# First head's output gate as a fifth column tile of the raw-input stage, with the small weights loaded later and the first head's decays and the recurrences' start steps renumbered

## The chip, the core and the metric

The kernel runs on one core of one Trainium2 chip. The metric is the device time of one execution in microseconds (us), as the median of several runs. The profile of one further execution, with all engines' instructions, is what the prediction reads. The engines are called by their short names: PE (TensorE, matrix products), PEld (its weight loads), DVE (VectorE), ACT (ScalarE), POOL (GpSimd) and SP (SyncE, which here only issues transfers); SPq, ACTq and POOLq are the queues from which transfers are issued.

## The reference, cut to what matters

One residual block on x of shape 512 x 1024. Two token mixers run side by side on the normalised input: a gated delta rule with eight heads of 128, and a convolution module. Then come merging gates and a SwiGLU channel mixer.

```
h = rmsnorm(x, norm1_w)
q, k, v, z, b_raw, a_raw, glu, gates = split(h @ w_in)
q, k, v = silu(causal_conv4([q, k, v]));  q, k = l2norm(q), l2norm(k)
beta = sigmoid(b_raw);  g = -exp(A_log) * softplus(a_raw + dt_bias)
o = gated_delta_rule(q, k, v, g, beta)          # per head, in chunks
out_a = (rmsnorm(o, dn_norm_w) * silu(z)) @ dn_w_o
ga, gb = split(glu + b_glu);  c = causal_conv31(ga * sigmoid(gb))
out_b = silu(layernorm(c)) @ cm_w_pw2
x = x + (gate_a * out_a + gate_b * out_b) @ w_out
x = x + (silu(f_gate) * f_up) @ ffn_w_down      # f from rmsnorm(x)
```

`z` is the gate of the heads' outputs, 128 columns for each head. `b_raw` and `a_raw` are 16 columns in all, and every head's decay and beta come from them.

## The kernel before, in words

All large products are done in three terms: each operand is split into a high and a low part, and `split3` (L112 to L118) issues high by high, high by low and low by high. `unit` (L98 to L110) loads 128 x 1024 weights with SP into `raw` (L105), makes the high part `whi` on ACT (L108) and the low part `wlo` on DVE (L109). These three tiles come from the pool `wp`, three buffers each, so a conversion has to wait until PE is through with the unit three before. One projection `proj(j)` is one unit and 24 matmuls of 128 x 512 on L118, given out in eight steps of three.

**The raw-input stage** (L205 to L302). The first four column tiles (the halves of the first two GLU pairs) are multiplied with the input before it is normalised, since the norm is one factor for each token that can be applied behind the product. `xt` comes in eight slices; ACT makes `uh` (L254), DVE makes `ul` (L255), and for every second slice three quarters of weights are converted (L260, L261). The 16 columns of `b_raw` and `a_raw` are done in the same loop (L265, L266) with the weights `wb`, which SP loads (L230) and DVE splits (L246, L247). Meanwhile the norm's factor `rsb` is made. Then the fourth tile is done alone (PSUM tile `b`), and the normalised input `hh` (ACT L299) and `hl` (DVE or POOL in turns, L300) is written slice by slice.

**The decays** (L304 to L339, L701 to L719). From the 16 columns DVE and ACT make `g` (written on L335) and `beta` in a chain of about 20 small operations. `decays` is a generator that starts two steps into the projections: it multiplies `g` with constant masks on PE (L707), takes exponentials on ACT, multiplies again (L714), copies the result on ACT into `mr` (L716, tile `cv`), and SP writes that to memory (`mrow`, L718). `decay(h)` reads a row of it back for head h, broadcast to 128 partitions (tile `DT`, L391), and makes the mask of decays on POOL and ACT (L393, L396).

**A head.** `head` (L721) projects and convolves k, q and v, and projects z (L737). `front` (L399) builds the triangular matrix of the head (`Un`, L422), writes its small diagonal blocks to memory and reads them back broadcast (SP, `sc` L437 and `U` L440), and POOL inverts these 16 x 16 blocks in 15 pairs of dependent operations (L454, L456; result `y`). `chain` then works from `y`: six small groups of matmuls on PE (L490, L496, L514, L522, L534, L539), with copies on DVE or ACT between them, give the whole inverse; four recurrence steps follow, each with L552/L553 (state), L555 (DVE, `R`), L558, L560 (ACT, `w`), L563/L564 and L570 (DVE, the new state). Everything in a chain depends on the piece before it.

**What sets the order.** The projections of heads and other tiles stand in a queue and are taken step by step (L665, `count`). `chains` holds the generators of `decays` and of the heads' `chain`; a number that a generator yields is the count of steps until it goes on. A head's chain is put in at step `START + 32 h + ...` (L771). That gives the program order with priorities; a scheduler at build time then sets the final order of each engine, within the dependences and its own estimate of readiness. `behind` and `issue_after` keep some operations behind others: POOL's part of `front` for head h + 1 stands behind the last operation of head h's inversion (`last`). On the chip each engine works through its own list in order, so that an instruction which waits holds up all behind it. `conv31` (L620, 30 operations on DVE for each of eight tiles, the first ACT L618 and the last ACT L622) fills DVE.

Of the kernel before, what the change touches and what calls it, by code (L numbers as in the profile page):

```python
# [14 lines left out]
P = 128  # L15
T = 512
NT = 4
# [4 lines left out]
OFF = 1600  # L22
PAD = 416
PAD3 = 368
START = 84
ROUND = 40
OTHERS = (12, 12, 12, 12, 8, 8, 8, 8)
EPS = 1e-6
# [3 lines left out]
def block_kernel(ctx, tc, a):  # L32
# [176 lines left out]
    with tc.tile_pool(name="st", bufs=2) as st:  # L209
# [5 lines left out]

        early = [[p.tile([P, 1024], dt, name=n, **kw) for dt, n in ((F32, "raw"), (F32R, "whi"), (F32R, "wlo"))]
                 for p, kw in ((wp, {}), (wp, {}), (st, {}), (st, {}))]
        nc.sync.dma_start(vec, a["vec"])
        nc.scalar.dma_start(ident, a["cst"][:, 0:P])

        def load(u, q):
            s = slice(256 * q, 256 * q + 256)
            nc.sync.dma_start(early[u][0][:, s], a["win"][(40, 32, 41, 33)[u]][:, s])

        for q in range(4):
            nc.sync.dma_start(xt[:, 2 * q, :], a["xt"][2 * q])
            load(0, q)
            nc.sync.dma_start(xt[:, 2 * q + 1, :], a["xt"][2 * q + 1])
            if q == 0:
                nc.sync.dma_start(wb, a["wba"])  # L230
            for u in (1, 2):
                load(u, q)
        xtok = pa_.tile([P, NT, D], F32, name="A")
        for n in range(NT):
            nc.sync.dma_start(xtok[:, n, :], a["x"][n])
# [7 lines left out]
        tc.cur_priority = prio  # L243
        wbhl = wbs[:, 0:2 * P].rearrange("p (k i c) -> p k i c", k=KD, i=2)
        wbh, wbl = wbhl[:, :, 0, :], wbhl[:, :, 1, :]
        V.tensor_copy(out=wbh, in_=wb)  # L246
        V.tensor_tensor(out=wbl, in0=wb, in1=wbh.bitcast(F32), op=ALU.subtract)  # L247


        bps = psg.tile([P, T], F32, name="g")  # L250
# [1 line left out]
        for k in range(KD):  # L252
            w = vec[:, k:k + 1]
            S.activation(uh[:, k, :], xt[:, k, :], AF.Copy, scale=w)  # L254
            V.scalar_tensor_tensor(out=ul[:, k, :], in0=xt[:, k, :], scalar=w, in1=uh[:, k, :].bitcast(F32),  # L255
                                   op0=ALU.mult, op1=ALU.subtract)
            if k % 2 == 0:
                c = slice(k * P, k * P + 256)
                for raw, hi, lo in early[:3]:
                    S.activation(hi[:, c], raw[:, c], AF.Copy)  # L260
                    V.tensor_tensor(out=lo[:, c], in0=raw[:, c], in1=hi[:, c].bitcast(F32), op=ALU.subtract)  # L261
            c = slice(k * P, k * P + P)
            for (_, hi, lo), ps in zip(early[:3], eps_):
                split3(ps, (hi[:, c], lo[:, c]), uh[:, k, :], ul[:, k, :], k == 0, k == KD - 1)
            PE.matmul(bps[0:32, :], wbs[:, 32 * k:32 * k + 32], uh[:, k, :], start=k == 0, stop=False)  # L265
            PE.matmul(bps[0:16, :], wbs[:, 32 * k:32 * k + 16], ul[:, k, :], start=False, stop=k == KD - 1)  # L266
        ss = st.tile([P, 2, NT], F32, name="rms_ss", bufs=1)
        for n in range(NT):
            S.activation(xtok[:, n, :], xtok[:, n, :], AF.Square, scale=1.0 / 32, accum_out=ss[:, 0, n:n + 1])
# [11 lines left out]
        for k in range(KD):  # L281
            c = slice(k * P, k * P + P)
            split3(eps_[3], (hi[:, c], lo[:, c]), uh[:, k, :], ul[:, k, :], k == 0, k == KD - 1)
        def glu0(i):
            sg = tp.tile([P, T], F32, name="sg")
            V.tensor_tensor(out=sg, in0=eps_[2 * i], in1=rsb, op=ALU.mult)
            S.activation(sg, sg, AF.Sigmoid, bias=b_glu[:, 8 + i:9 + i])
            c = tp.tile([P, T + 30], F32, name="c", bufs=3)
            V.memset(c[:, 0:30], 0.0)
            V.tensor_tensor(out=c[:, 30:], in0=eps_[2 * i + 1], in1=rsb, op=ALU.mult)  # L290
            V.scalar_tensor_tensor(out=c[:, 30:], in0=c[:, 30:], scalar=b_glu[:, i:i + 1], in1=sg,
                                   op0=ALU.add, op1=ALU.mult)
            cs.append(c)
# [13 lines left out]
        for n in range(NT):  # L307
# [24 lines left out]
        V.tensor_tensor(out=t0, in0=t0, in1=u, op=ALU.mult)  # L332
        V.tensor_tensor(out=sp, in0=sp, in1=t0, op=ALU.subtract)
        V.scalar_tensor_tensor(out=sp, in0=ax, scalar=0.0, in1=sp, op0=ALU.max, op1=ALU.add)
        V.tensor_tensor(out=g, in0=sp, in1=nea.rearrange("p (a h) -> p a h", a=1).broadcast_to([P, NT, H]),  # L335
                        op=ALU.mult)
        V.tensor_scalar(out=eb, in0=eb, scalar1=1.0, scalar2=None, op0=ALU.add)
        V.reciprocal(out=beta, in_=eb)
        V.tensor_scalar(out=nbeta, in0=beta, scalar1=-1.0, scalar2=None, op0=ALU.mult)  # L339


    gp = ph1.enter_context(tc.tile_pool(name="gp", bufs=1))
# [33 lines left out]
        yield  # L376
        return o

    zall = pa_.tile([P, H, T], F32, name="A")
    junk = tp.tile([P, T], F32, name="pa", bufs=1)  # L380

    def tok(src, pool, tag):
# [317 lines left out]

    def decays():  # L701

        yield 2
        gps = psg.tile([P, 4, P], F32, name="g")
        fl = lambda t: t.rearrange("p n h -> p (n h)")
        for i, m in enumerate((tri, suf, ones, mid)):
            PE.matmul(gps[:, i, 0:32], m, fl(g), start=True, stop=True)  # L707
        S.activation(fl(egc), gps[:, 0, 0:32], AF.Exp)
        S.activation(fl(kdf), gps[:, 1, 0:32], AF.Exp)
        S.activation(fl(egl), gps[:, 2, 0:32], AF.Exp)  # L710
        V.tensor_scalar(out=negc, in0=egc, scalar1=-1.0, scalar2=None, op0=ALU.mult)
        V.tensor_scalar(out=fl(nmc), in0=gps[:, 3, 0:32], scalar1=-1.0, scalar2=None, op0=ALU.mult)
        mps = psg.tile([P, 4, P], F32, name="g")
        PE.matmul(mps[0:32, 0, :], fl(g), mid, start=True, stop=True)  # L714
        mr = mrt[0:32, 0:P]
        S.activation(mr, mps[0:32, 0, :], AF.Copy)  # L716
        for n in range(NT):
            nc.sync.dma_start(mrow[:, n, :], mr[n * H:(n + 1) * H])  # L718
        dts.append(decay(0))  # L719

    def head(h, done):  # L721

        k_ = yield from conv4(8 + h, "kT")
        close()
        q_ = yield from conv4(h, "qT")
        close()
        v = conv4(16 + h, "vT")
        for _ in range(2):
            next(v)
            yield  # L730
        DT = dts.pop(0)
        if h + 1 < H:
            dts.append(decay(h + 1))
        with behind(), tc.issue_after(last[0].ins) if h else nullcontext():
            ss, kd, b2, Un, Ud, y = front(h, k_, DT)
        v_ = yield from v
        pz = yield from proj(24 + h)  # L737
        z_ = zall[:, h, :]
        S.activation(z_, pz, AF.Silu)

# [27 lines left out]
    nh = 0  # L768
    while step() or chains:
        start_feed[0] = count[0] >= 335  # L770
        if nh < H and count[0] >= START + 32 * nh + sum(OTHERS[:nh]):  # L771
            chains.append([0, chain(*done[nh])])
            nh += 1
        for c in list(chains):
            if c[0] <= count[0] or not queue:
                with behind():
                    n = next(c[1], None)
                if n is None:
                    chains.remove(c)
                else:  # L780
                    c[0] = count[0] + n
# [515 lines left out]
```

## Time and profile before

| what | us |
|---|---|
| median of three runs | 963.14 |
| lowest and highest run | 960.74, 963.42 |
| the profiled execution | 964.17 |
| its span in the trace | 961.9 |
| PE busy | 941.8 (98%) |
| DVE busy | 731.8 (76%) |
| ACT busy | 529.4 (55%) |
| POOL busy | 357.4 (37%) |

Of the profiled execution 2.3 us lie outside the span. Rows of the timeline read: start in us, duration in us, engine, line, operation, the tile written and the tile read, partitions x elements, and a count where like rows in a run are put together. In brackets at the end stands how long the engine sat idle before, and what ended that. Matmuls are pipelined, so that a matmul's duration is longer than the distance to the next start; that distance, the pitch, is what counts. A matmul of plain 32-bit numbers shows as two records (x8 for four of them), a three-term matmul of L118 as one.

### The profile page before, as it was taken

Reading aid. Unit: us, or ns where it says so; the run is one execution under the profiler, and the core shown is the slowest. Engines: PE = TensorE matmul, PEld = TensorE weight load, DVE = VectorE, ACT = ScalarE, POOL = GpSimd, SP = SyncE. Lnnn points to the kernel's source line nnn. Section 1 sums busy time; section 2 is a strip of 40 time slices with the busy share of each in tenths; the row PEclk is TensorE's granted clock in tenths of the full one; section 3 lists DMA queues with packets and bytes.
Section 4 is the critical chain, followed back from the end, with each engine's and each line's share of the span. In section 5 each row is a group of like instructions: output and inputs, shape, how many; then the busy total and the mean of one; then the engine's idle time right before and its main releaser. Section 6 shows DMA issues by size and latency. Waiting matters only on the chain.

```text
span 961.9 us, 14869 instructions
## 1 busy us (share of the span) xinstructions
PE 941.8 (98%) x5199; PEld 793.8 (83%) x5199; DVE 731.8 (76%) x1118; ACT 529.4 (55%) x1095; POOL 357.4 (37%) x565
## 2 busy tenths in 40 slices
PE   6999999999999999999999999999999999999996
PEld 5687888888887887888887888888889999988885
DVE  4898888988888888888477763676525887889886
ACT  6588865867856775544547232423324545556554
POOL 0323645243463327534345342245451111134034
PEclk9999999999999999999999999999999999999999
DMA  9243423133231426988897985499899556578653
GB/s 310 94 143 101 123 66 92 59 116 102 66 103 55 129 82 176 279 253 248 257 297 221 288 277 175 174 272 281 294 252 224 191 184 193 174 221 268 212 192 134
DMA packets 78298, 177.39 MB, mean 184 GB/s; under 512 B 10208, under 2 KB 19328, under 8 KB 77200
## 3 DMA queue, kind: packets, MB, share of 16 engines
q1 hardware_dynamic: 66816, 144.88, 45.4%
q0 software_dynamic: 10256, 28.89, 13.3%
q10 hardware_dynamic: 1152, 2.69, 0.7%
q8 instruction: 41, 0.67, 0.3%
q14 instruction: 33, 0.27, 0.1%
HBM read 156.22 MB, written 45.37 MB: 210 GB/s over the span
## 4 chain that ended last, share of the span: by engine, by line
PE 90%; DVE 4%; ACT 2%; POOL 2%; issue 1%; DMA 1%; SPq 0%; POOLq 0%; ACTq 0%; DVEq 0%
PE mm L118 59%; PE w L118 20%; PE g L385 1%; PE st L564 1%; PE g L418 1%; PE st L558 1%; DVE wlo L109 1%; PE b L490 1%; PE st L563 1%; PE b L496 1%; DMA gsl<-sgd 1%; POOL ss L879 1%; PE b L514 1%; PE st L552 1%; PE g L467 1%
## 5 line engine op out<-in xcount | busy, mean ns | idle before, releaser
L108 ACT ACTIVATE whi<-raw 128x1024 fp32r<-128x1024 f32 (+1 forms) x191 | 196.4, 1030 | 246.8 <-PE mm L118 151.1
L109 DVE TENSOR_TENSOR wlo<-raw,whi 128x1024 fp32r<-128x1024 f32 (+1 forms) x191 | 242.3, 1270 | 95.9 <-ACT whi L108 95.3
L118 PE MATMUL mm<-hh,whi 128*128 128x512 f32 (+1 forms) x688 | 269.9, 393 | 0.5 <-ACT whi L108 0.3
L118 PE MATMUL mm<-hl,whi 128*128 128x512 f32 (+1 forms) x688 | 264.0, 384 | 2.3 <-POOL hl L300 1.6
L118 PE MATMUL mm<-hh,wlo 128*128 128x512 f32 (+1 forms) x688 | 263.9, 384 | 0.1
L620 DVE SCALAR_TENSOR_TENSOR cps<-c,c31w,cps 128x512 f32<-128x512 f32 x240 | 180.2, 751 | 4.3
L118 PEld LDWEIGHTS mm<-hl,whi 128*128 128x128 f32 x688 | 129.9, 189 | 24.7 <-POOL hl L300 2.9
L118 PEld LDWEIGHTS mm<-hh,wlo 128*128 128x128 f32 x688 | 129.6, 188 | 23.8 <-DVE wlo L109 0.6
L118 PEld LDWEIGHTS mm<-hh,whi 128*128 128x128 f32 x688 | 129.8, 189 | 22.7 <-ACT whi L108 0.8
L949 POOL TENSOR_TENSOR fm<-fm 128x256 f32<-128x256 f32 x33 | 29.8, 904 | 113.3 <-DVE s L949 90.1
L372 DVE SCALAR_TENSOR_TENSOR acc<-mm,c4w,acc 128x511 f32<-128x511 f32 (+2 forms) x72 | 53.0, 738 | 1.9 <-ACT acc L369 1.9
L118 PE MATMUL mm<-yh,whi 128*128 128x512 f32 x128 | 50.7, 396 | 0.0
L118 PE MATMUL mm<-yl,whi 128*128 128x512 f32 x128 | 50.0, 391 | 0.6 <-DVE yl L808 0.6
L454 POOL TENSOR_TENSOR ytm<-U,y 128x60 f32<-128x60 f32 (+14 forms) x120 | 31.8, 265 | 48.6 <-DMA U<-sc 30.9
L118 PE MATMUL mm<-yh,wlo 128*128 128x512 f32 x128 | 49.8, 389 | 0.0
L118 PE MATMUL w<-hh,wlo 128*128 128x256 f32 x168 | 47.7, 284 | 0.3 <-DVE wlo L109 0.3
L118 PE MATMUL w<-hh,whi 128*128 128x256 f32 x168 | 47.6, 284 | 0.0
L118 PE MATMUL w<-hl,whi 128*128 128x256 f32 x168 | 47.5, 283 | 0.0
L118 PE MATMUL w<-wlo,fh 128*128 128x512 f32 (+1 forms) x115 | 44.3, 385 | 0.2 <-DVE wlo L109 0.2
L118 PE MATMUL w<-whi,fl 128*128 128x512 f32 (+1 forms) x115 | 44.2, 384 | 0.0
L118 PE MATMUL w<-whi,fh 128*128 128x512 f32 (+1 forms) x115 | 44.2, 384 | 0.0
L456 POOL TENSOR_TENSOR y<-y,ytm 128x60 f32<-128x60 f32 (+14 forms) x120 | 39.0, 325 | 9.4
(324 smaller groups left out, 1904.0 us busy)
## 6 DMA issues: line engine op xcount, KB each, us to landing
raw<-in_win_dram SPq DMA_DIRECT2D x61, 512.0 KB, 3.5
raw<-in_wgu_dram SPq DMA_DIRECT2D x32, 512.0 KB, 3.5
s<-in_wgu_dram SPq DMA_DIRECT2D x48, 256.0 KB, 6.2
raw<-s SPq DMA_DIRECT2D x48, 256.0 KB, 3.8
raw<-wsum SPq DMA_DIRECT2D x44, 256.0 KB, 4.0
raw<-in_wdn_dram SPq DMA_DIRECT2D x33, 256.0 KB, 3.3
s<-in_wgu_dram POOLq DMA_DIRECT2D x24, 256.0 KB, 6.9
s<-s POOLq DMA_DIRECT2D x24, 256.0 KB, 7.0
```

The costliest lines, as they stand in the source:

```text
L108: marked(S.activation(hi, raw, AF.Copy), "unit")
L109: marked(V.tensor_tensor(out=lo, in0=raw, in1=hi.bitcast(F32), op=ALU.subtract), "unit")
L118: marked(PE.matmul(ps, l, r, start=first and i == 0, stop=last and i == 2))
L372: marked(V.scalar_tensor_tensor(out=acc[:, s:], in0=ps[:, :T - s], scalar=c4w[:, j, k:k + 1], in1=acc[:, s:], op0=ALU.mult, op1=ALU.add))
L385: PE.transpose(ps[:, n, :], src[:, n, :], ident)
L418: PE.matmul(ps[:, n, :], kT[:, n, :], kT[:, n, :], start=True, stop=True)
L454: G.tensor_tensor(out=tm[:, :, 0:w], in0=U[:, k, :, k + 1:], in1=y[:, :, k:k + 1].broadcast_to([P, NT, w]), op=ALU.mult)
L456: last[0] = G.tensor_tensor(out=y[:, :, k + 1:], in0=y[:, :, k + 1:], in1=tm[:, :, 0:w], op=ALU.add)
L467: PE.matmul(ps[:, n, :], kT[:, n, :], qT[:, n, :], start=True, stop=True)
L490: PE.matmul(ps[:, n, 0:16], Ud[:, n, :], xc[:, n, 0:16], start=True, stop=True)
L620: V.scalar_tensor_tensor(out=acc, in0=c[:, k:k + T], scalar=c31w[:, i, k:k + 1], in1=acc, op0=ALU.mult, op1=ALU.add)
L949: return eng.tensor_tensor(out=out, in0=in0, in1=in1, op=op)
```

## The change

- `vec` is loaded from ACT's queue and not SP's, so that the first slice of `xt` is SP's first transfer. `wb` is loaded after the three quarters of weights of the first round, and its split on DVE stands in the loop's second pass. The matmuls with it follow two slices later, so that PE's first instruction is a projection on L118.
- Column tile 24 (z of head 0) becomes a fifth tile on the raw input, into the PSUM tile `st`, straight behind the fourth. DVE multiplies it with `rsb` behind the operation that writes `g`, and ACT applies Silu. Head 0 has no z projection any more, and is eight steps shorter.
- `decays` starts twelve steps into the projections and not two.
- `START` is 80 and not 84, and heads 1 to 7 get four steps off, for the steps that head 0 no longer has.

```diff
-START = 84
+START = 80
...
-        nc.sync.dma_start(vec, a["vec"])
+        nc.scalar.dma_start(vec, a["vec"])
...
+            for u in (1, 2):
+                load(u, q)
             if q == 0:
                 nc.sync.dma_start(wb, a["wba"])
-            for u in (1, 2):
-                load(u, q)
...
-        V.tensor_copy(out=wbh, in_=wb)
-        V.tensor_tensor(out=wbl, in0=wb, in1=wbh.bitcast(F32), op=ALU.subtract)
...
-            PE.matmul(bps[0:32, :], wbs[:, 32 * k:32 * k + 32], uh[:, k, :], start=k == 0, stop=False)
-            PE.matmul(bps[0:16, :], wbs[:, 32 * k:32 * k + 16], ul[:, k, :], start=False, stop=k == KD - 1)
+            if k == 1:
+                V.tensor_copy(out=wbh, in_=wb)
+                V.tensor_tensor(out=wbl, in0=wb, in1=wbh.bitcast(F32), op=ALU.subtract)
+            for b in [k - 2] if 1 < k < KD - 1 else [k - 2, k - 1, k] if k > 1 else []:
+                PE.matmul(bps[0:32, :], wbs[:, 32 * b:32 * b + 32], uh[:, b, :], start=b == 0, stop=False)
+                PE.matmul(bps[0:16, :], wbs[:, 32 * b:32 * b + 16], ul[:, b, :], start=False, stop=b == KD - 1)
...
+        zps = pst.tile([P, 4, P], F32, name="st").rearrange("p n t -> p (n t)")
+        hi, lo = unit(a["win"][24])
+        for k in range(KD):
+            c = slice(k * P, k * P + P)
+            split3(zps, (hi[:, c], lo[:, c]), uh[:, k, :], ul[:, k, :], k == 0, k == KD - 1)
+        zall = pa_.tile([P, H, T], F32, name="A")
...
+        with tc.issue_after(g_.ins):
+            V.tensor_tensor(out=zall[:, 0, :], in0=zps, in1=rsb, op=ALU.mult)
+        S.activation(zall[:, 0, :], zall[:, 0, :], AF.Silu)
...
-        yield 2
+        yield 12
...
-        pz = yield from proj(24 + h)
         z_ = zall[:, h, :]
-        S.activation(z_, pz, AF.Silu)
+        if h:
+            pz = yield from proj(24 + h)
+            S.activation(z_, pz, AF.Silu)
...
-        if nh < H and count[0] >= START + 32 * nh + sum(OTHERS[:nh]):
+        if nh < H and count[0] >= START + (32 * nh - 4 if nh else 0) + sum(OTHERS[:nh]):
```

The final order of the engines moves further than the diff says. The first place is ACT's list around the copy of the decays, `cv_99<-g` 32x128 (`mr`). In the kernel before it stands on L716, right behind the last exponential of the decays, with six weight conversions (L108) of `unit` ahead of it in the list:

```order
L710 ACTIVATE sm_414<-g_488 128x32
L716 ACTIVATE cv_99<-g_498 32x128
L375 ACT_TABLE_LOAD
L375 ACTIVATE vT_780<-acc4_775 128x512
L405 ACTIVATE pa_454,ss_659<-g_660 128x128
L739 ACTIVATE A_453<-mm_782 128x512
```

In the changed kernel the same copy stands on L728, behind the end of the second tile's 31-tap convolution (L634, before L622):

```order
L752 ACTIVATE A_398<-mm_1557 128x512
L108 ACTIVATE whi_1847<-raw_1846 128x1024
L634 ACTIVATE cv_102<-cps_576 128x512
L728 ACTIVATE cv_99<-g_642 32x128
L382 ACTIVATE acc4_1832<-mm_1747,c4w_79 128x512
L108 ACTIVATE whi_1902<-raw_1901 128x1024
```

So 19 weight conversions of `unit` now stand ahead of the copy. The matmul that feeds it (L714, now L726) has hardly moved on PE: 187 matmuls of L118 were ahead of it, and now 180 are. The first chain's first matmul on PE (L490, now L502) had 354 matmuls of L118 ahead of it and now has 631, the second chain's 487 and now 672, the third's 618 and now 707.

The second place is PE's list in the recurrences of head 0. In the kernel before, pieces of a chain stand between matmuls of the projections (`hh`, `hl` with `whi`, `wlo`), as here in one recurrence step of head 0, where `st_1532<-R` and the `st_1532<-w` that waits for it have six of these between them:

```order
L118 MATMUL mm_1559<-hl_92,whi_1561 128x512
L118 MATMUL mm_1559<-hh_91,wlo_1562 128x512
L558 MATMUL st_1532<-R_1535,Y_437 128x128
L118 MATMUL mm_1559<-hh_91,whi_1561 128x512
L118 MATMUL mm_1559<-hl_92,whi_1561 128x512
L118 MATMUL mm_1559<-hh_91,wlo_1562 128x512
L118 MATMUL mm_1559<-hh_91,whi_1561 128x512
L118 MATMUL mm_1559<-hl_92,whi_1561 128x512
L118 MATMUL mm_1559<-hh_91,wlo_1562 128x512
L563 MATMUL st_1532<-w_1547,kd_669 128x128
L564 MATMUL st_1532<-w_1547,at_848 128x128
```

In the changed kernel the last three steps of head 0 stand without a projection between them, and the first matmul of head 1's chain (L502) follows in the same stretch:

```order
L118 MATMUL mm_2336<-hh_91,wlo_2339 128x512
L570 MATMUL st_1542<-R_1545,Y_471 128x128
L575 MATMUL st_1542<-w_1571,kd_702 128x128
L576 MATMUL st_1542<-w_1571,at_849 128x128
L564 MATMUL st_1600<-S_1584,kT_541 128x128
L565 MATMUL st_1600<-S_1584,qT_670 128x128
L570 MATMUL st_1600<-R_1603,Y_471 128x128
L575 MATMUL st_1600<-w_1622,kd_702 128x128
L576 MATMUL st_1600<-w_1622,at_849 128x128
L564 MATMUL st_1695<-S_1661,kT_541 128x128
L565 MATMUL st_1695<-S_1661,qT_670 128x128
L502 MATMUL b_1700<-xc_1671,Ud_1039 128x16 x4
```

Behind the last row the stretch goes on without a projection through all six small groups of head 1's inverse, to L551 (before L539). The next projection's matmul (`mm_2397`) comes after that, with no matmul of L118 between it and `mm_2336`.

More of the change, by code (lines that the diff above doesn't have):

```diff
@@ L334, in block_kernel @@
         V.scalar_tensor_tensor(out=sp, in0=ax, scalar=0.0, in1=sp, op0=ALU.max, op1=ALU.add)
-        V.tensor_tensor(out=g, in0=sp, in1=nea.rearrange("p (a h) -> p a h", a=1).broadcast_to([P, NT, H]),
+        g_ = V.tensor_tensor(out=g, in0=sp, in1=nea.rearrange("p (a h) -> p a h", a=1).broadcast_to([P, NT, H]),
                         op=ALU.mult)
@@ L377, in conv4 @@
         return o
-    zall = pa_.tile([P, H, T], F32, name="A")
     junk = tp.tile([P, T], F32, name="pa", bufs=1)
```

## The prediction

> **What bounds the kernel now.** I read the page first, then the list of waits with PE's own rows, then the timelines around the edits, and last the build order shown above. The page's engine line, its chain by engine and the longest waits of PE:
>
> ```profile
> PE 941.8 (98%) x5199; PEld 793.8 (83%) x5199; DVE 731.8 (76%) x1118; ACT 529.4 (55%) x1095; POOL 357.4 (37%) x565
> ...
> PE 90%; DVE 4%; ACT 2%; POOL 2%; issue 1%; DMA 1%; SPq 0%; POOLq 0%; ACTq 0%; DVEq 0%
> ```
>
> ```profile
> PE g L265 <- DVE cv L247: 7.2, 1, 7.2
> PE mm L118 <- POOL hl L300: 1.6, 2, 1.3
> ...
> PE mm L118 <- DVE hl L300: 0.6, 1, 0.6
> ```
>
> PE is the bound: 941.8 of 961.9 us busy. The change takes no matmul away (the z tile moves, all 24 remain), so only PE's idle time can move, and of the 20.1 us that are idle 7.2 lie before the first matmul and 2.2 in two names of one stall. What the change could gain is small. What it could lose is any wait that it makes on PE, since each stands one to one in the time. Therefore I look for new waits as carefully as for removed ones.
>
> **The start.** The timeline of the first microseconds, with PE's pitch until it quickens:
>
> ```profile
> 0.73 0.40 SPq L218 DMA_DIRECT2D vec<-in_vec_dram  x1
> ...
> 1.18 0.42 SPq L226 DMA_DIRECT2D xt<-in_xt_dram  x1
> ...
> 4.14 1.28 ACT L254 ACT_TABLE_LOAD   x1 [4.14 <-DMA xt<-in_xt_dram]
> ...
> 5.44 0.72 ACT L254 ACTIVATE uh<-xt,vec 128x512 fp32r<-128x512 f32 x1
> ...
> 6.07 0.40 ACT L260 ACTIVATE whi<-raw 128x256 fp32r<-128x256 f32 x1
> ...
> 7.22 0.61 PE L265 MATMUL g<-uh,cv 128*32 128x512 f32 x1 [7.22 <-DVE cv L247]
> ...
> 7.63 0.63 PE L118 MATMUL mm<-uh,whi 128*128 128x512 f32 x1
> ...
> 12.75 0.63 PE L118 MATMUL mm<-uh,wlo 128*128 128x512 f32 x1
> 13.17 0.44 PE L118 MATMUL mm<-uh,whi 128*128 128x512 f32 x1
> 13.45 0.40 PE L118 MATMUL mm<-ul,whi 128*128 128x512 f32 x1
> ```
>
> `vec` off SP's queue lets `xt` go one slot earlier (0.73 in place of 1.18), 0.45 us. ACT's chain of table load, `uh` and `whi` follows it: `whi` ended at 6.47 and would end at 6.02, and PE, whose first product is now on L118, would start 0.13 later for its weights, at about 6.15 and not 7.22. That is **-1.1**. Moving `wb` and its split costs nothing there, as the first product with it comes 27 matmuls later. The pitch is 0.42 up to 13.17 and then about 0.24 (0.28 for the first). If the quickening stays at 13.17, only the 2.5 matmuls that fit into 1.07 us are gained at the fast pitch, 0.6; if all 13 slow matmuls were fast, 13 x 0.19 = 2.5 would come on top of 1.1. So -0.6 to -3.6; I take the plain shift, since the transfers of the next slices set these rows as well.
>
> The Trainium skill ("TensorE: Matmul & The Clock Gate", Part 1) says that the clock opens after a busy window of about 3.4 us that runs free of the kernel's start; by that the gain here would be the 0.6, or about 2.8 if a whole window were saved.
>
> **The z tile over the stall.** PE's rows where the normalised input is written:
>
> ```profile
> 37.08 0.50 PE L118 MATMUL mm<-hh,whi 128*128 128x512 f32 x1
> ...
> 41.34 0.50 PE L118 MATMUL mm<-hl,whi 128*128 128x512 f32 x1 [1.29 <-POOL hl L300]
> ...
> 46.29 0.50 PE L118 MATMUL mm<-hl,whi 128*128 128x512 f32 x1 [0.36 <-POOL hl L300]
> ...
> 46.85 0.40 PE L118 MATMUL mm<-hh,whi 128*128 128x512 f32 x1
> ```
>
> A long undisturbed piece of the chain that ended last, for the pitch, and the last piece of `hl`:
>
> ```profile
> 91.44 11.17 PE mm L118 x49
> ```
>
> ```profile
> 44.94 1.29 POOL L300 TENSOR_TENSOR hl<-xt,hh 128x512 fp32r<-128x512 f32 x1 [1.96 <-ACT hh L299]
> ```
>
> The undisturbed pitch is 11.17 / 49 = 0.228. From 37.08 to 46.85 PE took 27 steps, so 6.2 of the 9.8 us were work and 3.6 a stall, more than the 2.2 in the list of waits, since small gaps aren't listed. The 24 matmuls of the z tile, 5.5 us, need no `hl` and now stand there. With the start 1.1 earlier, PE would come to the first `hh` product at about 41.4 and to the last slice of `hl` at 46.4. The z tile's weight conversion (L109) also stands on DVE ahead of the `hl` chain, which ended at 46.23 and would end at about 46.5 (1.1 earlier for the start, 1.3 later for the conversion). So nearly all of the stall is covered: **-3.5** (0 if the chain slips by as much as the tile takes, -3.6 at most).
>
> **The wait for g.** DVE's chain from the sixteen columns to `g`, PE's reader, and the mean durations of what stands between on DVE:
>
> ```profile
> 45.92 0.21 DVE L309 COPY cv<-g 128x64 f32<-128x64 f32 x1
> ...
> 60.82 0.19 DVE L335 TENSOR_TENSOR cv<-cv 128x32 f32<-128x32 f32 x1
> ```
>
> ```profile
> 61.40 0.97 PE L707 MATMUL g<-cv,cst 128*128 128x32 f32 x8
> 62.30 0.41 PE L714 MATMUL g<-cst,cv 128*32 128x128 f32 x2
> ```
>
> ```profile
> L109 DVE TENSOR_TENSOR wlo<-raw,whi 128x1024 fp32r<-128x1024 f32 (+1 forms) x191 | 242.3, 1270 | 95.9 <-ACT whi L108 95.3
> L620 DVE SCALAR_TENSOR_TENSOR cps<-c,c31w,cps 128x512 f32<-128x512 f32 x240 | 180.2, 751 | 4.3
> L372 DVE SCALAR_TENSOR_TENSOR acc<-mm,c4w,acc 128x511 f32<-128x511 f32 (+2 forms) x72 | 53.0, 738 | 1.9 <-ACT acc L369 1.9
> ```
>
> PE was just behind `g` (61.01 against 61.40). The changed PE list has 60 matmuls of L118 between the first `hh` product and the reader, where it had 91: 41.4 + 60 x 0.228 = 55.1. DVE's new list has between the same two ends two L109, ten of the 0.75 us kind and 16 small ones: 2.5 + 10 x 0.66 (they overlap a little) + 16 x 0.1 (the next starts while one ends) = 10.7, from about 46.4, so 57.1. PE waits **+2** (0 to 4); the projection after it in PE's list stands behind this wait.
>
> **The late copy of the decays.** The chain before, from the copy to the first two inversions and the first chain's matmul:
>
> ```profile
> 62.74 0.27 ACT L716 ACTIVATE cv<-g 32x128 f32<-32x128 f32 x1
> ```
>
> ```profile
> 91.26 0.99 POOL L454 TENSOR_TENSOR ytm<-U,y 128x60 f32<-128x60 f32 x1 [8.96 <-DMA raw<-in_win_dram]
> ...
> 102.56 0.21 POOL L456 TENSOR_TENSOR y<-y,ytm 128x4 f32<-128x4 f32 x1
> ...
> 129.20 0.21 POOL L456 TENSOR_TENSOR y<-y,ytm 128x4 f32<-128x4 f32 x1
> ...
> 162.50 0.21 POOL L456 TENSOR_TENSOR y<-y,ytm 128x4 f32<-128x4 f32 x1
> ```
>
> ```profile
> 108.35 0.96 PE L490 MATMUL b<-xc,Ud 128*128 128x16 f32 x8
> ```
>
> From the copy at 62.74 to `y` of head 0 (102.77) it was 40.0 us, to head 1's another 26.6, and from the start of POOL's part for head 2 (the row below) to the end of its `y` 24.6:
>
> ```profile
> 138.15 1.04 POOL L412 TENSOR_TENSOR ss<-ss,root 128x4 f32<-128x4 f32 x1 [8.74 <-DVE ss L410]
> ```
>
> In the new list the copy stands behind 19 weight conversions and the end of a 31-tap convolution. The last of these conversions needs PE to be through with the projection three units before, which has 480 matmuls of L118 ahead of its end, 300 of them after the reader of `g`: 57.1 + 300 x 0.228 + some 4 for the small groups between, at up to 1 us each as L707's row has it, = 130. Then one conversion on ACT (1.1), one on DVE (1.3), the six last taps (6 x 0.66) and two short ACT copies: 136.9. The way from there to `y` of head 0 took 40 us; POOL's 8.96 us of waiting at 91.26, put down to a load of weights, may shrink, so 35 to 40, and I take 35: **172**. Heads 1 and 2 follow 26.6 and 24.6 later, since their part of POOL stands behind the inversion before: 198.6 and 223.2. What lies between `y` and the chain's first matmul is two ACT copies and a transpose; I take 3 us (5.6 at 108.35).
>
> PE's own arrival, by its list at the pitches above: at the first chain 172, at the second 190, at the first projection behind the bare stretch 196.4, at the third chain 209.4. Against the readiness of 175, 201.6 and 226.2, PE waits 3 at the first and stands some 17 later at the third. Part of this is the bare stretch itself, where a recurrence step takes its full latency:
>
> ```profile
> 143.13 0.39 PE L552 MATMUL st<-S,kT 128*128 128x128 f32 x2
> 144.18 0.49 PE L558 MATMUL st<-R,Y 128*128 128x128 f32 x2
> 145.13 0.49 PE L563 MATMUL st<-w,kd 128*128 128x128 f32 x2
> ```
>
> Between these rows lie 1.05 and 0.95 us for 0.45 of PE's work, and no projection hides it now. The two accounts overlap (the wait for `y` runs beside the recurrence), and give the same: 201.6 at head 1's first matmul, then its bare inverse of six groups (0.8 to 0.9 us each, an estimate from the 0.96 of L490) and five hops (0.95 as above, up to 1.6 where several copies stand between, an estimate), 9.5 to 13 us, so PE is at the next projection at 211 to 215 and not 196.4. I take **+16.5** (from +5.6, if only hops count and `y` is never late, to +22 with 40 us to the first `y`). Behind the stretch I add **+1** for weights whose loads SP issues behind this stretch's transfers. ACT gets five more table loads (5 x 1.28), hidden as it is 55% busy.
>
> **The sum:** -1.1 - 3.5 + 2 + 16.5 + 1 = +14.9 against the profiled 964.17, hence 979.1. That execution lies 1.0 above the median of the runs, 963.14, so I predict **978**.
>
> **The rivals.**
>
> *The recurrences stay covered (not slower).* If the inversions of heads 1 and 2 follow within 15 us of the one before, `y` is there whenever PE comes, and only the start's and z tile's gains stand against the wait for `g`: -4.6 + 2, 960 to 963. For it: ACT's part of `front` can be ready long before, as the projections run ahead. Against: the 26.6 and 24.6 us above are POOL's own list and its transfers. It decides at 15 us of period. 12 in 100, half under 960.2.
>
> *A smaller stall.* The hops count but POOL's period falls to 18, since transfers have less before them: third chain ready at 172 + 36 + 3 = 211 against 209.4, bare hops +5.6, in all +3 to +8: 966 to 971. 18 in 100.
>
> *PE's clock falls in the stretch.* PE would then be idle for about 6 us in one piece (own arrival and hops 195.5, `y` 201.6). The longest idle time that the rows above show behind the start is 1.29, and the pitch after it is as before, so the trace can't tell. If PE came back at the pitch of the start, 0.42, for as long as it did there (5.5 us), it would cost about 2.5 more: 980 to 984. 20 in 100. The Trainium skill (same page and Part) has the clock halved after one idle window of about 3.4 us; the trace neither shows nor excludes it.
>
> **The numbers.** The forecast, 972 to 982 without that clock, has 50 in 100. The range of 966 to 985 leaves out the first rival and a little at the top, where 40 us to `y` and the clock come together. About 0.3% (2.9 us) is what a measurement of this kernel can tell from no change: faster 0.06, same 0.07, slower 0.87.
>
> **What would show it.** Right: PE's first matmul at about 6.2 on L118; no `hl` wait over 0.5; a wait of PE for `g` of about 2; ACT's copy L728 near 137; `y` of head 0 near 172; and a list of waits with some 15 us on the chain's lines (L502, L526, L570, L575) between 172 and 215. Wrong: the copy before 100, or the second `y` less than 18 after the first.

## The result, and the profile after

The changed kernel takes 985.76 us (median of 4 runs, 985.41 to 988.63), the kernel before 963.03 in the runs beside it (4 runs, 960.74 to 963.42). The ratio is 1.0241, with a 95% interval of 1.0213 to 1.0269: slower by 2.4%. The forecast was 978 with a range of 966 to 985. The direction and the late copy came out; PE's path behind the copy did not, and the time is 7.8 us above the forecast and 0.8 above the range. The profiled execution has a span of 983.4 where the kernel before had 961.9, 21.5 more.

The page's engine line and the chain by engine, as shown of the kernel before:

```profile
PE 949.5 (97%) x5199; PEld 804.8 (82%) x5199; DVE 740.0 (75%) x1119; ACT 535.0 (54%) x1100; POOL 351.8 (36%) x561
...
PE 83%; POOL 5%; DVE 3%; DMA 3%; issue 2%; ACT 2%; SPq 1%; POOLq 0%; ACTq 0%; DVEq 0%
```

PE is busy 7.7 us longer with the same 5199 matmuls, so part of them ran slower, and it is idle 13.8 us longer. POOL has 5% of the chain where it had 2%, and DMA 3% where it had 1%: the chain now passes through the inversions. The longest waits of PE:

```profile
PE mm L118 <- ACT whi L258: 6.1, 1, 6.1
PE st L564 <- DVE o L589: 4.0, 2, 2.2
PE g L397 <- ACT pa L484: 2.9, 1, 2.9
PE mm L118 <- ACT sg L616: 1.9, 1, 1.9
PE g L719 <- issue: 1.9, 1, 1.9
PE g L479 <- ACT Un L433: 1.7, 1, 1.7
```

The wait at the start is shorter, those for `hl` are gone, the wait for `g` (L719) is there with 1.9, and the other four lines are new. Three of these are waits for ACT (L397, L118 and L479, 6.5 in all) and were not in the forecast. Of the 15 us or so that the forecast put on L502, L526, L570 and L575 between 172 and 215 only 1.6 are there.

The start, the first product of the normalised input and the reader of `g`, on PE's timeline:

```profile
6.08 0.79 PE L118 MATMUL mm<-uh,whi 128*128 128x512 f32 x1 [6.08 <-ACT whi L258]
...
10.13 0.40 PE L118 MATMUL mm<-uh,whi 128*128 128x512 f32 x1
...
40.57 0.50 PE L118 MATMUL mm<-hh,whi 128*128 128x512 f32 x1
...
56.38 1.05 PE L719 MATMUL g<-cv,cst 128*128 128x32 f32 x8 [1.92 <-issue]
...
57.70 0.65 PE L118 MATMUL mm<-hh,whi 128*128 128x512 f32 x1
58.15 0.63 PE L118 MATMUL mm<-hl,whi 128*128 128x512 f32 x1
58.58 0.63 PE L118 MATMUL mm<-hh,wlo 128*128 128x512 f32 x1
```

PE starts at 6.08 (forecast 6.15) and quickens at 10.13, not at 13.17. Less the z tile's 24 matmuls (5.5 us) the first product of `hh` is at 35.1, 2.0 earlier than before. The reader of `g` waits 1.92 as forecast. What was not forecast is the row behind it: the pitch is 0.43 and not 0.228. PE runs at half speed for the next eight matmuls.

ACT's late copy and the ends of the first three inversions on POOL:

```profile
130.21 1.06 ACT L108 ACTIVATE whi<-raw 128x1024 fp32r<-128x1024 f32 x1 [3.89 <-PE mm L118]
137.37 0.60 ACT L634 ACTIVATE cv<-cps 128x512 f32<-128x512 f32 x1 [6.10 <-DVE cps L632]
137.86 0.25 ACT L728 ACTIVATE cv<-g 32x128 f32<-32x128 f32 x1
```

```profile
173.27 1.09 POOL L468 TENSOR_TENSOR y<-y,ytm 128x4 f32<-128x4 f32 x1
...
197.14 0.21 POOL L468 TENSOR_TENSOR y<-y,ytm 128x4 f32<-128x4 f32 x1
...
219.91 0.21 POOL L468 TENSOR_TENSOR y<-y,ytm 128x4 f32<-128x4 f32 x1
```

The copy starts at 137.86 (forecast 136.9), and the inversions end at 174.4, 197.4 and 220.1 (forecast 172, 198.6, 223.2). PE's first matmuls of the first two chains and what lies between:

```profile
161.50 0.66 PE L397 MATMUL g<-cst,kT 128*128 128x128 f32 x4 [2.90 <-ACT pa L484]
...
164.08 0.80 PE L118 MATMUL mm<-hh,whi 128*128 128x512 f32 x1 [1.92 <-ACT sg L616]
...
180.44 0.96 PE L502 MATMUL b<-xc,Ud 128*128 128x16 f32 x8
...
198.43 0.39 PE L576 MATMUL st<-w,at 128*128 128x128 f32 x2
200.62 0.49 PE L564 MATMUL st<-S,kT 128*128 128x128 f32 x2 [1.79 <-DVE o L589]
...
207.43 1.73 PE L502 MATMUL b<-xc,Ud 128*128 128x16 f32 x8
```

Here the forecast departs: 180.44 in place of 175, and 207.43 in place of 201.6. Neither of these matmuls has a wait of its own in its row, and at 207.43 `y` had been ready for 10 us. PE came late to both.

### The profile page after: what moved, and what is told of

Read it like the earlier page. It is cut to its first block, busy times and chain, and to the rows that moved or that the text cites. A ratio compares the mean times of both kernels' runs of the same rounds, so it can differ in the third digit from the quotient of the medians.

```text
span 983.4 us, 14899 instructions
## 1 busy us (share of the span) xinstructions
PE 949.5 (97%) x5199; PEld 804.8 (82%) x5199; DVE 740.0 (75%) x1119; ACT 535.0 (54%) x1100; POOL 351.8 (36%) x561
## 4 chain that ended last, share of the span: by engine, by line
PE 83%; POOL 5%; DVE 3%; DMA 3%; issue 2%; ACT 2%; SPq 1%; POOLq 0%; ACTq 0%; DVEq 0%
PE mm L118 55%; PE w L118 19%; POOL y L468 1%; POOL ytm L466 1%; DVE wlo L109 1%; SPq L452 1%; PE g L397 1%; DMA U<-sc 1%; DMA raw<-s 1%; PE st L570 1%; PE st L576 1%; POOL ss L891 1%; PE b L118 1%; PE st L118 1%; PE g L479 1%
## 5 line engine op out<-in xcount | busy, mean ns | idle before, releaser
L108 ACT ACTIVATE whi<-raw 128x1024 fp32r<-128x1024 f32 (+1 forms) x191 | 196.6, 1030 | 262.6 <-PE mm L118 172.1
L118 PE MATMUL mm<-hh,whi 128*128 128x512 f32 (+1 forms) x680 | 267.1, 393 | 1.9 <-ACT sg L616 1.9
L118 PE MATMUL mm<-hh,wlo 128*128 128x512 f32 (+1 forms) x680 | 263.2, 387 | 0.0
L118 PE MATMUL mm<-hl,whi 128*128 128x512 f32 (+1 forms) x680 | 263.1, 387 | 0.0
L118 PEld LDWEIGHTS mm<-hh,whi 128*128 128x128 f32 x680 | 129.7, 191 | 23.7 <-ACT sg L616 2.2
L118 PEld LDWEIGHTS mm<-hh,wlo 128*128 128x128 f32 x680 | 129.4, 190 | 22.9
L118 PEld LDWEIGHTS mm<-hl,whi 128*128 128x128 f32 x680 | 129.7, 191 | 21.3
L385 DVE SCALAR_TENSOR_TENSOR acc<-mm,c4w,acc 128x509 f32<-128x509 f32 (+2 forms) x72 | 53.2, 742 | 10.3 <-ACT acc L382 10.1
L118 PE MATMUL mm<-yh,whi 128*128 128x512 f32 x128 | 50.8, 397 | 0.0
L118 PE MATMUL mm<-yl,whi 128*128 128x512 f32 x128 | 50.1, 391 | 0.2 <-DVE yl L820 0.2
L466 POOL TENSOR_TENSOR ytm<-U,y 128x60 f32<-128x60 f32 (+14 forms) x120 | 34.0, 284 | 44.6 <-DMA U<-sc 35.8
L118 PE MATMUL mm<-yh,wlo 128*128 128x512 f32 x128 | 49.9, 390 | 0.0
L118 PE MATMUL w<-hh,wlo 128*128 128x256 f32 x168 | 47.9, 285 | 1.0 <-DVE wlo L109 1.0
L118 PE MATMUL w<-hh,whi 128*128 128x256 f32 x168 | 47.7, 284 | 0.0
L118 PE MATMUL w<-hl,whi 128*128 128x256 f32 x168 | 47.6, 283 | 0.0
L118 PE MATMUL w<-wlo,fh 128*128 128x512 f32 (+1 forms) x115 | 44.4, 386 | 0.2 <-DVE wlo L109 0.2
L118 PE MATMUL w<-whi,fl 128*128 128x512 f32 (+1 forms) x115 | 44.3, 385 | 0.0
L118 PE MATMUL w<-whi,fh 128*128 128x512 f32 (+1 forms) x115 | 44.3, 385 | 0.0
L169 POOL TENSOR_TENSOR wst<-wst 128x512 f32<-128x512 f32 x20 | 31.8, 1592 | 28.4 <-DMA wst<-in_wdn_dram 27.2
```

The source lines that it names most:

```text
L108: marked(S.activation(hi, raw, AF.Copy), "unit")
L118: marked(PE.matmul(ps, l, r, start=first and i == 0, stop=last and i == 2))
L169: G.tensor_tensor(out=o, in0=x, in1=y, op=ALU.add)
L385: marked(V.scalar_tensor_tensor(out=acc[:, s:], in0=ps[:, :T - s], scalar=c4w[:, j, k:k + 1], in1=acc[:, s:], op0=ALU.mult, op1=ALU.add))
L466: G.tensor_tensor(out=tm[:, :, 0:w], in0=U[:, k, :, k + 1:], in1=y[:, :, k:k + 1].broadcast_to([P, NT, w]), op=ALU.mult)
```

## The experiments

All are compared with the kernel before on the same chip, whose median was 963.2 to 963.3.

### Where the loss comes from: the place of one copy

Theory: the loss is the place of the decays' copy in ACT's list. Rivals: the chains that start four steps sooner have too little beside them, or PE's clock. Three kernels tell these apart. The first is the kernel before with one number changed:

```diff
-        yield 2
+        yield 12
```

> The kernel before with twelve in place of two in decays and nothing else. The build order then has the copy behind 19 weight conversions, and the first three chains after 633, 672 and 705 matmuls of L118. LATE COPY: the whole loss without the gains of the other parts, 963.1 + 20 to 25 = 983 to 988. COVER: within 3 us of 963, as START, the start and the z tile are those of the kernel before.

Measured: 987.11 us (985.36 to 988.42), ratio 1.0245 (1.0228 to 1.0261). One number gives the whole loss, with the old START, the old start and the z projection where it was. Its copy on ACT:

```profile
136.78 0.60 ACT L622 ACTIVATE cv<-cps 128x512 f32<-128x512 f32 x1 [4.77 <-DVE cps L620]
137.28 0.25 ACT L716 ACTIVATE cv<-g 32x128 f32<-32x128 f32 x1
```

It stands behind the end of the same convolution, at 137.28. The second kernel keeps the twelve steps and all of the change, and takes the copy's tile out of the pool in which the convolutions' results lie:

```diff
-        mr = mrt[0:32, 0:P]
+        mr = small.tile([32, P], F32, name="mr")
```

> The changed kernel with one line different: the copy of the decays (mr) gets a tile of its own and no longer a piece of the pool tile mrt that it shares with the convolution's results. All else stays, the twelve steps, START = 80 and the z tile among it. In the build order the copy then has 6 weight conversions of ACT ahead of it (19 in the changed kernel, 6 before), and the first three chains start after 363, 483 and 615 matmuls of L118 on PE (631, 672, 707 in the changed kernel). Theory LATE COPY (the loss is the place of the copy alone, which comes from that tile): the 24.9 us that the changed kernel loses behind PE's reader of g go, and the start's and z tile's gains stay, so 959 to 962. Rival COVER (chains that start four steps sooner, with eight steps fewer in head 0, have too little beside them wherever the copy stands): at least 970, with waits of PE on the recurrences' lines. Rival CLOCK (PE's idle time at the reader of g starts a series of slow stretches): 975 or more, since that wait of about 2 us stays.

Measured: 963.77 us (10 runs, 961.97 to 966.6), ratio 1.0009 (0.9997 to 1.002). The copy is early again:

```profile
59.70 0.26 ACT L728 ACTIVATE mr<-g 32x128 f32<-32x128 f32 x1
```

So the twelve steps do harm only through the tile, and neither the four steps nor the wait for `g` makes the loss of 22 us. The third kernel is the change with two steps:

```diff
-        yield 12
+        yield 2
```

> The changed kernel with the decays two steps on, as before, in place of twelve. The copy then has 6 weight conversions ahead of it again. LATE COPY: 959 to 962, and within 2 us of the kernel with the copy's own tile. COVER: at least 970. A rival of its own, that twelve steps are worth something by keeping PE from waiting for g: 2 to 4 us more than with the copy's own tile; the build order has the reader of g after 179 matmuls of L118, against 180, which speaks against it.

Measured: 963.54 us (959.17 to 969.52), ratio 1.0008 (0.9988 to 1.0029), the same as with the own tile. That twelve steps save PE a wait is not borne out; the wait for `g` is 1.9 in both kernels.

In both kernels with the late copy it stands directly behind the end of a 31-tap convolution. Why a tile from the same pool ties it there, these runs don't show, nor at which number of steps between two and twelve the copy moves.

The own tile and the two steps both miss the 959 to 962 that the theory gave, by somewhat under 2 us. The gains of start and z tile had gone somewhere.

### The two gains, one by one

The start alone, on the kernel before:

```diff
-        nc.sync.dma_start(vec, a["vec"])
+        nc.scalar.dma_start(vec, a["vec"])
...
+            for b in [k - 2] if 1 < k < KD - 1 else [k - 2, k - 1, k] if k > 1 else []:
+                PE.matmul(bps[0:32, :], wbs[:, 32 * b:32 * b + 32], uh[:, b, :], start=b == 0, stop=False)
```

> The kernel before with the new start alone: vec on ACT's queue, the small weights later, their matmuls two slices later. Chains stand where they did (354, 487, 618). The predicted term was -1.1 (-0.6 to -3.6); the changed kernel's trace has PE at its first products of the normalised input 2.0 us further on when the z tile's 24 matmuls are taken off. So 961.1 if all of it reaches the end, 962.0 by the predicted shift, 963.1 if the stall at the normalised input swallows it.

Measured: 962.67 us (961.36 to 964.08), ratio 0.9995 (0.9985 to 1.0004). It can't be told from no change. In its profile PE is 2.1 us ahead at the first product of `yh` (477.5 against 479.6) and 0.9 ahead at the last of `hh` in the gate and up stage (838.4 against 839.3).

The change without the new start and with two steps, which leaves the z tile and the renumbered chains:

```diff
-        nc.scalar.dma_start(vec, a["vec"])
+        nc.sync.dma_start(vec, a["vec"])
...
-        yield 12
+        yield 2
```

> The changed kernel with the start of the kernel before and two steps for the decays: the z tile as a fifth tile and the renumbered chains alone. FEED and the cover of the hl stall: PE is 3.6 us further on behind the stall, less 1.9 for the wait for g, less what a halved clock behind that wait costs (1.6), so level or 1 us ahead there, and the sums start one unit late, which costs 0 to 3 us: 963 to 966. If the cover of the stall reaches the end: 959 to 961.

Measured: 966.93 us (965.69 to 969.32), ratio 1.0044 (1.0028 to 1.0061): 0.9 above the expected band. PE is 2.9 us ahead at the first `yh` (476.7) and behind at the end of the gate and up stage (841.5). So both gains arrive in the middle of the kernel and are given back later. PE's milestones (first number of the pair: first start; second: last start) for the kernel before and for the own tile, from the source view of L118:

```profile
L118 PE MATMUL mm<-yh,whi x128: 388/389/796, 479.6 to 569.0; 128*128 128x512 f32 x128
...
L118 PE MATMUL w<-hh,whi x168: 277/283/364, 615.8 to 839.3; 128*128 128x256 f32 x168
```

```profile
L118 PE MATMUL mm<-yh,whi x128: 388/389/796, 476.3 to 565.4; 128*128 128x512 f32 x128
...
L118 PE MATMUL w<-hh,whi x168: 278/283/387, 612.2 to 842.8; 128*128 128x256 f32 x168
```

From 615.8 to 839.3 the kernel before takes 223.5 us, the own tile from 612.2 to 842.8 takes 230.6: 3.6 ahead turn into 3.5 behind. (This profiled run, 966.6, is the slowest of its ten, but the two kernels above with the z tile and two steps, with and without the new start, need 229.5 and 229.1 in theirs.) What ACT waits for between 700 and 780, in the kernel before and with the own tile (in total, times, longest):

```profile
ACT whi L108 <- DMA raw<-s: 3.3, 4, 1.5
```

```profile
ACT whi L108 <- DMA raw<-s: 16.9, 8, 6.3
```

`raw<-s` are weights loaded from sums that the kernel builds in memory beforehand. The building begins at step 335 of the queue, and head 0 now has eight steps fewer, so that step 335 lies one weight unit further on in the work.

### The sums one unit sooner

```diff
-        start_feed[0] = count[0] >= 335
+        start_feed[0] = count[0] >= 327
```

on the kernel with the own tile.

> The changed kernel with the copy's own tile (963.8 us where it was measured) and with the step at which the queue begins to build sums of the later gate and up weights in memory (start_feed) at 327 and not 335. Head 0 has eight steps fewer, so step 335 falls one weight unit later in the work than before. Theory FEED (the gains of start and z tile, 3.3 us at the first matmul of the merging stage, are given back between 720 and 770, where PE waits for weights whose raw tile is loaded from those sums, 8 waits of ACT on raw<-s with 16.9 us against 4 with 3.3 before): one unit sooner brings 2 to 4 us, 960 to 962. Rival BANDWIDTH (the transfers of that stretch are the bound whatever their order, so PE waits there however early it comes): 963 to 964, no change. Rival CLOCK: the loss comes from a slow stretch of PE there that an idle time of another cause sets off, no change.

Measured: 961.90 us (11 runs, 960.59 to 963.0), ratio 0.9988 (0.9979 to 0.9997): 1.9 less than without it, and faster than the kernel before by little more than its interval. The stage's milestones and ACT's wait between 700 and 780:

```profile
L118 PE MATMUL w<-hh,whi x168: 277/283/364, 613.1 to 837.1; 128*128 128x256 f32 x168
```

```profile
ACT whi L108 <- DMA raw<-s: 6.6, 4, 4.1
```

The stage takes 224.0. One unit sooner again:

```diff
-        start_feed[0] = count[0] >= 335
+        start_feed[0] = count[0] >= 319
```

> As feed_327, with step 319, one weight unit earlier again. FEED: the same as with 327 or up to 2 us less (959 to 962). BANDWIDTH: 963 to 964. If the earlier sums crowd out other weights, it is slower than 327.

Measured: 961.75 us (959.71 to 963.85), ratio 0.9983 (0.9973 to 0.9993), not to be told from 327. A second unit brings nothing more. The same edit on the changed kernel, with the copy still late:

```diff
-        start_feed[0] = count[0] >= 335
+        start_feed[0] = count[0] >= 327
```

> The changed kernel with step 327 in place of 335 for the sums, and nothing else; the copy stands late as in the changed kernel. If the changed kernel's time is the sum of a late copy and a late start of the sums (it needs 225.3 us from the first to the last product of hh in the gate and up stage, the kernel before 223.5), it falls by about 2, to 983.5 to 984.5. If the sums only matter where PE comes early (as in the kernel with the copy's own tile, 230.6 us there), no change: 985 to 986.5.

Measured: 984.55 us (984.18 to 986.47), ratio 1.0224 (1.0208 to 1.0239). That is 1.2 below the changed kernel, between the two expected bands, and the intervals overlap: as a time inconclusive. In the profiles the stage does get shorter, 223.4 (637.0 to 860.4) against 225.3, and ACT's wait for `raw<-s` from 600 to 870 falls from 12.7 to 2.4. But PE comes to the stage 1.4 later, with a wait of 1.7 for `yl` (L820) ahead of it that is 0.2 in the changed kernel.

### PE's clock in the stretch

PE's granted clock in the changed kernel, by windows (us, then busy times of PE, PEld, DVE, ACT, POOL with counts, PEclk, DMA share, GB/s):

```profile
200.00:205.00 5.00, 2.73 (x10) 1.95 (x10) 3.64 (x8) 3.76 (x18) 4.54 (x10) 0.62 0.52 166
205.00:210.00 5.00, 3.59 (x17) 3.60 (x18) 3.95 (x8) 4.25 (x12) 0.83 (x1) 0.50 0.44 105
```

The clock does fall. Whether that costs time is tried with 32 matmuls more in the recurrence of head 0, in three places of each step:

```diff
+        def warm(n):
+            if h == 0:
+                fb = psb.tile([P, 4, P], F32, name="b").rearrange("p n t -> p (n t)")
+                for _ in range(n):
+                    PE.matmul(fb, hh[:, 0, 0:P], hh[:, 0, :], start=True, stop=True)
...
+                warm(2)
                 yield 3
...
             PE.matmul(ps[:, 1, :], Y[:, n, :], R, start=True, stop=True)
+            warm(2)
...
+            if n < NT - 1:
+                warm(6)
```

> The changed kernel with 32 matmuls of 128 x 512 more in the recurrence steps of head 0 (2 behind each product with the state, 2 behind each product with the inverse, 6 behind the last product of each of three steps; they multiply hh with itself into a tile that nobody reads), 7.3 us of PE work at its pitch of 0.228. The order puts them into the stretch without projections. Theory CLOCK (PE's clock, granted at half between 201 and 215 and between 218 and 226 in the changed kernel, costs several us since PE is busy through 208 to 214): PE keeps its full clock there and the time is 979 to 984 in spite of the added work. Rival LATENCY (the time of that stretch is that of the chain of operations and of POOL's inversions, the clock costs nothing): 985 to 990.

Measured: 985.37 us (984.04 to 987.67), ratio 1.0232 (1.0213 to 1.0252). The same windows:

```profile
200.00:205.00 5.00, 5.00 (x28) 3.89 (x26) 4.34 (x10) 3.93 (x18) 4.28 (x7) 1.00 0.25 74
205.00:210.00 5.00, 4.26 (x30) 3.62 (x28) 4.47 (x9) 4.83 (x13) 0.90 (x3) 1.00 0.29 92
```

PE is busy nearly throughout, at the full clock, and its first matmul of head 1's chain comes at 207.13 in place of 207.43. From the first chain's first matmul (181.35, against 180.44) that is 25.8 in place of 27.0. So 7.3 us of added work and a full clock together make this piece 1.2 shorter and the kernel no different, as the rival had it that the chain's latency sets the time up to 207. What the clock alone is worth there, without the added work, this run does not separate. Behind 210 the clock fell in both kernels (0.66, 0.74 and 0.58 in the windows from 210 to 225 of this one), so that what it costs there, where the first projection runs at half pitch, stays open.

### Four steps later

The best version so far with the old START:

```diff
-START = 80
+START = 84
```

on the kernel with the own tile and step 327.

> The kernel with the copy's own tile and step 327 (961.9 us) with START = 84 in place of 80, so that all chains stand four steps later. The first four chains then have 379, 495, 627 and 759 matmuls of L118 ahead (363, 483, 615, 747 with 80), and ACT 46 table loads in place of 36. If the four steps are worth what they are meant for, 962.5 to 964; if the chains had time to spare, 961 to 962.5; if ten more table loads (1.28 us each) reach PE, above 964.

Measured: 958.47 us (6 runs, 956.87 to 960.49), ratio 0.9951 (0.9937 to 0.9965). All three expected bands are wrong: four steps later is better, by 3.4 us against START = 80, and the ten table loads more cost nothing that shows. This version beats both kernels. Of PE's waits over half a microsecond in the recurrences, START = 80 has one:

```profile
PE b L526 <- DVE Xd L514: 0.7, 1, 0.7
```

which is gone with 84. So with the copy early the START = 80 of the change was a loss of its own. In the windows from 60 to 450 PE was idle for 0.4 us with 84 and for 1.7 with 80, and 1.0 of the difference between these two profiles lies ahead of 41, where the edit can't act. The rest isn't settled.

## Why the prediction was right in kind and short in size

**The start, -1.1.** -2.0 at the first product of `hh`. The shift of 1.07 came as 1.14 (6.08), and the clock opened 4.05 us after the first matmul in place of 5.95. So the plain shift was too small, but part of the row is luck. In the nine profiles with the new start the first matmul of L118 lies between 5.98 and 6.20, and the pitch falls from 0.43 to under 0.33 between 8.76 and 11.75; in the kernel with twelve steps alone, which has the old start, it falls at 11.11 and not 13.17, and the first product of `hh` comes at 35.9, 1.2 earlier than in the kernel before. This fits the Trainium skill's account ("TensorE: Matmul & The Clock Gate", Part 1) of a window that runs free of the kernel's start.

**The z tile, -3.5.** The waits for `hl` are gone, and the 3.6 us with them. Right.

**The wait for g, +2.** 1.92. Right, but what it does to the clock was missing: eight matmuls at a pitch of 0.43, 1.6 us.

```profile
58.00:60.00 2.00, 2.00 (x6) 1.51 (x6) 2.00 (x3) 1.95 (x6) 1.47 (x6) 0.50 0.16 20
```

The rival on the clock had looked at the stretch only, and for an idle time of 6 us. 1.9 was enough here. In the kernel with the z tile and the renumbered chains but neither the new start nor the twelve steps (the run z_early) a wait of 1.95 changed nothing:

```profile
58.00:60.00 2.00, 2.00 (x14) 1.62 (x14) 1.84 (x6) 1.16 (x5) 1.56 (x6) 1.00 0.06 18
```

Of the nine kernels' profiles with this wait, it is the only one of full clock from 56 to 66; the other eight have a mean of 0.83 there. The Trainium skill ("TensorE: Matmul & The Clock Gate", Part 1) asks for an idle window of about 3.4 us. The trace differs: a wait of 1.9 us was followed by a half clock, for about 3.4 us.

**The late copy, +16.5: the mis-sized term.** That the copy's place makes the loss is shown by the three kernels above, and the copy and the first three inversions came within 3.1 us of their times. From PE's reader of `g` (56.38 against 61.40; 3.4 us ahead, less the seven matmuls of L118 that now come behind it) to the first `yh` (19.9 behind: 499.5 against 479.6) the changed kernel lost 23.3, of which 1.6 is the clock behind `g`: 21.7 in place of 16.5 + 1. The step that failed is "at the first chain 172", PE's own arrival. I took PE's list at its pitches up to there, and let it wait for nothing but `y`: 114.9 us from the reader of `g` (57.1) to 172, where it took 124.1 (56.38 to 180.44). The late copy releases the masks of three heads at once and of a fourth soon after, and ACT's list has their exponentials, with a table load at each change of function, ahead of what PE needs:

```profile
147.34 1.28 ACT L408 ACT_TABLE_LOAD   x1
148.86 2.54 ACT L408 ACTIVATE DT<-DT,sm 128x128 f32<-128x128 f32 x8 [0.24 <-POOL DT L405]
...
155.91 1.28 ACT L388 ACT_TABLE_LOAD   x1
...
157.86 1.28 ACT L408 ACT_TABLE_LOAD   x1
...
162.04 1.28 ACT L616 ACT_TABLE_LOAD   x1
163.34 0.69 ACT L616 ACTIVATE sg<-mm,vec 128x512 f32<-128x512 f32 x1
```

PE's waits of 1.7, 2.9 and 1.9 for ACT end at 155.95, 161.50 and 164.08, and PE comes to the first chain at 180.44. These 6.5 us, the half clock behind `g` (1.6) and another half clock behind the wait at 164.08 (seven matmuls in 3.1 us, 1.5 too long) are the 9.2 us that were missing, within 0.4. "Hidden as it is 55% busy" was said of ACT's table loads by an average over the kernel; between 154 and 164 ACT was busy for 9.9 of 10 us and PE for 3.6 (order of the columns as above):

```profile
154.00:164.00 10.00, 3.55 (x22) 2.40 (x20) 8.78 (x13) 9.91 (x26) 2.99 (x7) 0.99 0.27 74
```

The trace shows this, and no experiment took it away by itself.

The second part of that step also failed. I had `y` of head 1 setting the second chain (201.6); it was ready at 197.4, and the bare recurrence of head 0 set it. From PE's first matmul of the first chain to that of the second I had 23.5 us (172 to 195.5), and it took 27.0. The hops that I took at 1.05 and 0.95 took 1.15 and 1.25 in the step from 200.62. The hop from one step's last products to the next step's first, for which I showed no row, took 2.19 (198.43 to 200.62), since DVE has weights and a convolution tap in its list between the two pieces that the hop needs:

```profile
198.23 1.22 DVE L109 TENSOR_TENSOR wlo<-raw,whi 128x1024 fp32r<-128x1024 f32 x1
199.36 0.34 DVE L582 SCALAR_TENSOR_TENSOR S<-S,sm,st 128x128 f32<-128x128 f32 x1
199.62 0.75 DVE L632 SCALAR_TENSOR_TENSOR cps<-c,c31w,cps 128x512 f32<-128x512 f32 x1
200.28 0.28 DVE L589 TENSOR_TENSOR o<-st,R 128x128 f32<-128x128 f32 x1
```

The row of L564 names `o` (L589) as what it waited for: the next step's products go to the one `st` tile, which `o` must have been read from first. The next such hop took 2.80 (203.61 to 206.41), with 2.16 of waiting for `o` in its row.

**Behind the stretch, +1.** The gate and up stage took 225.3 in place of 223.5, 1.8, but from the sums that begin one unit late, which the prediction did not see: the edit that shortens head 0 moves a threshold that counts steps. With the threshold moved back the stage takes 223.4, as in the kernel before; that the kernel's time follows is shown for the early copy only.

**The rivals.** *Covered recurrences* fell with the result. *A smaller stall* fell: POOL's period was 23.0 and 22.8 and not 18. *The clock* did fall in the stretch, without an idle time of 6 us in one piece; that figure had also left out the 3 us that PE was to wait at the first chain. The full clock and the added matmuls together brought 1.2 us up to 207; behind 210 its price is open. Behind `g` a half clock cost 1.6, where I had 2.5 for the stretch.

The forecast's parts against the measured ones, by profile: start -2.0 (-1.1), z tile -3.6 (-3.5), wait 1.9 (2), clock behind it 1.6 (0), late copy 21.7 (17.5 with the loads behind the stretch), sums 1.8 (0). Together 21.4, and the spans differ by 21.5. The parts are differences between milestones of two single executions, so that they have to add up to about this; the start's part has luck of about 1 us in it, and the late copy's part holds the half clocks from 164 on.

## What to carry to other kernels

When one copy on an in-order engine moves back, don't price its own chain alone: list all that it releases at once and what then stands in each engine's list between that and the next thing PE needs. A number that counts steps (a start, a threshold) is an edit to every place that counts, and a gain that shows in the middle of the kernel can be given back at the next stage's transfers: look at milestones, not only at the end. If a scheduler moves an instruction further than the code, look at the tile it shares before changing its step.

## What the runs showed of the hardware

A wait of PE of 1.92 us was followed by 3.4 us at half clock (pitch 0.43 from 57.70 to 61) in the changed kernel, and one of 1.95 in another kernel (z_early) by none. In the stretch PE was busy for all of 210 to 215 while its clock was granted at 0.51:

```profile
210.00:215.00 5.00, 5.00 (x36) 4.78 (x36) 3.36 (x10) 3.43 (x11) 3.62 (x13) 0.51 0.00 0
```

so that a busy share of 1.00 there is work at half speed. A change of ACT's function took 1.30 from the load to the next activation (155.91 to 157.21).
